# Scaling softmax blocks out of the score bank, and one float32 product with v per head and key block in two column groups

## The chip, the cores and the metric

The kernel runs on one core of a Trainium2 chip. The core has five engines with queues of their own: TensorE (PE, with weight loads shown apart as PEld), VectorE (DVE), ScalarE (ACT), GpSimd (POOL) and SyncE (SP, which issues the transfers here). PE writes its products to PSUM, eight banks of 128 partitions x 512 float32 numbers; everything else lies in SBUF. The metric is the time of one execution on the device in microseconds (us).

## The reference

Two layers of a decoder trunk on 512 positions of width 1024, all float32. Layer 0 has stick-breaking attention, layer 1 forgetting attention; each is followed by a gated MLP with a short convolution.

```python
for i in range(DEPTH):                       # 2 layers; i = 0 stick-breaking, i = 1 forgetting
    h = modulate(rmsnorm(x, g_mix_pre[i]), sh_a, sc_a)
    q, k, v = split(h @ w_qkv[i])            # 16 heads of 64
    # i = 0: a = sigmoid(z) * prod over later keys of (1 - sigmoid(z)), strictly causal
    # i = 1: a = softmax(z + cum[t] - cum[s]), causal, cum = cumsum(log_sigmoid(h @ w_fg + b_fg))
    o = (a @ v) @ w_o[i]
    x = x + gt_a * rmsnorm(o, g_mix_post[i])
    h = modulate(rmsnorm(x, g_ffn_pre[i]), sh_f, sc_f)
    y = (silu(conv3(h @ w_gate[i])) * (h @ w_up[i])) @ w_down[i]
    x = x + gt_f * rmsnorm(y, g_ffn_post[i])
```

The modulation vectors come from `silu(c) @ w_mod[i] + b_mod[i]`.

## The kernel before

Most products are made of three (`mm3`): both operands are kept as a rounded high half and a low half of type float32r, and high x high, low x high and high x low are added in a bank. `split` makes the halves: ACT copies (the high half), DVE or POOL subtracts (the low half).

Attention goes head by head. For each of the four blocks of 128 queries (`qb` from 3 to 0, so 512, 384, 256 and 128 keys wide), `scores` makes two products into a bank `ps`. Layer 0 then calls `stick`, layer 1 `fox`: DVE adds the decay and takes the row's minimum (L461), ACT takes the exponential and its sum (L464), DVE the reciprocal (L465) and the scaling (L466). In `fox` all of it after the first step lies in an SBUF tile `fx`.

One head later, `transposed` turns the probabilities with PE into banks `pa`, one for each key block `kb` (512, 384, 256 and 128 queries wide), and `split` brings each to SBUF as `ah` and `al`. `weighted` then multiplies: for each key block two products, with `ah` and with `al` moving and a tile of v as the fixed operand that holds 64 columns of high halves and 64 of low halves of this head. So high and low parts of the result stand in the two halves of the bank `po`; ACT copies one half across (L496), DVE adds the other (L497), and after the second head of a pair `split` makes `oh` and `ol`.

The order on PE and SP is as written. Where the attention would wait, `fill` puts pieces of other products (projections `pqk` of the next pair, values `pv`, output projections into further `po` banks) between its steps; the table `UNITS` has how many pieces a head takes. In layer 0 also pieces of the modulation stand there: L202 makes eight float32 products, 32 columns each, at four column positions of the array. Within ACT, DVE and POOL a scheduler sets the order in the attention stages. All PSUM tiles come from one pool of eight banks, and most working tiles in SBUF from one pool of 44 slots.

Of the kernel before, what the change touches and what calls it, by code (L numbers as in the profile page):

```python
# [20 lines left out]
NH = 16  # L21
HD = 64
# [6 lines left out]
MULN = 256  # L29
# [8 lines left out]
def trunk(ctx, tc, x, c, w_mod, b_mod, g_mix_pre, g_mix_post, w_qkv, w_o, w_fg, b_fg,  # L38
          g_ffn_pre, g_ffn_post, w_gate, w_up, w_conv, b_conv, w_down, out):
    nc = tc.nc  # L40
# [22 lines left out]
    def tiny(s, n=1):  # L63
        return sb.tile([P, n], F32, tag=f"tiny{n}", name=nm(s), bufs=24)
# [180 lines left out]
    def split(hi, lo, src, engine=None):  # L245
        nc.scalar.copy(hi, src)  # L246
        (engine or nc.vector).tensor_tensor(lo, src, hi.bitcast(F32), op=ALU.subtract)  # L247
# [158 lines left out]
    A, B = slice(0, HD), slice(HD, P)  # L406
# [30 lines left out]
    def scores(l, hd, qb, q, k):  # L437
        n = (qb + 1) * P
        qs = slice(qb * P, n)
        ps = bank("ps")  # L440
        for i in range(2):
            nc.tensor.matmul(ps[:, :n], q[hd][:, qs], k[hd][i][:, :n], start=i == 0, stop=i == 1)  # L442
        return ps, n
# [11 lines left out]
        return bt  # L455

    def fox(ps, qb, cum):
        n = (qb + 1) * P
        t = slot("fx", F32)
        m, s, r = tiny("mx"), tiny("sm"), tiny("rc")  # L460
        nc.vector.tensor_tensor_reduce(  # L461
            t[:, :n].rearrange("p (b k) -> p b k", k=P), ps[:, :n].rearrange("p (b k) -> p b k", k=P), cum(qb),
            1.0, BIG, op0=ALU.add, op1=ALU.min, accum_out=m)
        nc.scalar.activation(t[:, :n], t[:, :n], AF.Exp, scale=-1.0, bias=m, accum_out=s)  # L464
        nc.vector.reciprocal(r, s)  # L465
        nc.vector.tensor_scalar(t[:, :n], t[:, :n], r, None, op0=ALU.mult)  # L466
        return t

    def transposed(probs):

        res = {}
        for kb in range(NT):
            n = (NT - kb) * P
            ps = bank("pa")
            for qb in range(NT - 1, kb - 1, -1):
                nc.tensor.transpose(ps[:, (qb - kb) * P : (qb - kb + 1) * P], probs[qb][:, kb * P : (kb + 1) * P], idn)  # L476
            if kb == 1:
                shared = slot("ah"), slot("al")
            hi, lo = (slot("ah"), slot("al")) if kb in (0, 2) else shared
            o = 384 if kb == 3 else 0  # L480
            hi, lo = hi[:, o : o + n], lo[:, o : o + n]
            split(hi, lo, ps[:, :n])
            res[kb] = (hi, lo)
            yield res

    def weighted(h, vt, at, o):

        po = bank("po")
        for kb in range(NT):
            lhs = by_head(vt[h // 4, kb])[:, h % 4, :]  # L490
            nc.tensor.matmul(po[:, kb * P :], lhs, at[kb][0], start=kb == 0, stop=False)
            nc.tensor.matmul(po[:, kb * P :], lhs, at[kb][1], start=False, stop=kb == NT - 1)
            yield
        hi, lo, f = o
        own, other = ((A, B), (B, A))[h % 2]
        nc.scalar.copy(f[own], po[other])  # L496
        nc.vector.tensor_tensor(f[own], po[own], f[own], op=ALU.add)  # L497
        if h % 2:
            split(hi, lo, f)

    def by_head(v):

        return v.rearrange("p (h e) -> p h e", h=4)

    def values(l, g, t, ht, vt):

# [70 lines left out]
    def drain(g):  # L577
        for _ in g:
            pass

    def attention(l, qk, vt, ot, filler, units, bg):


        get = cums_of.get(l)
        late, cums = None, {}
        for h in range(NH + 1):
            p, hd = divmod(h, 2)
            done = [0, 0]

            def fill(n=1):  # L590
                done[0] += n
                u = (units[h] * min(done[0], 12) + 11) // 12 - done[1]
                done[1] += u
                filler.run(u)

            if h < NH and hd == 0:
                ot.append((slot("oh"), slot("ol"), slot("of", F32)))
# [4 lines left out]
            probs, at = {}, None  # L602
# [12 lines left out]
            if late:  # L615
                drain(turned)
                for i, _ in enumerate(weighted(late[1], vt, at, ot[late[1] // 2])):
                    if i % 2:
                        fill()
            fill(12)  # L620
            late = (probs, h)
            if h:
                bg.step()


    def begin(vt, qk):
# [41 lines left out]
        part, xt, acc, H = {}, {}, [], S // 2  # L668
# [87 lines left out]
        r = stats(0)  # L756
# [4 lines left out]
        for t in range(NT):  # L761
            n = t + 1
# [29 lines left out]
        for j in range(ND):  # L792
            n = j + 1
# [17 lines left out]
        qk[0, 0] = queries(acc[4], 0.125)  # L811
        qk[0, 1] = keys(acc[6], kl[0])
        ws.upto(1)
        for g in range(2):
            for t in range(NT):
                keep_values(acc[t][:, 256 * g : 256 * g + 256], g, t, vt)
        qk[1, 0] = queries(acc[5], 0.125)
        return ht

# [1 line left out]
    for l in range(DEPTH):  # L821
        bg = Background([(l, GT_A), (l, SC_F), (l, SH_F)] if l == 0 else [], mod_part_pe)
        scale = -0.125 if l % 2 else 0.125
# [33 lines left out]
        gens, ot = [], []  # L857
        for p in range(1, NPAIR):
            if (l, p) == (0, 3):
                gens.append(conv_columns())  # L860
            gens += [proj(l, p, j, ht, s, qk) for j, s in ((0, scale), (1, None)) if (p, j) not in qk]
            if p % 2 == 0 and (p // 2, 0) not in vt:
# [66 lines left out]
        for f in range(2, NF):  # L929
            g, u = bank("pgu"), bank("pgu")  # L930
# [67 lines left out]
```

## Time and profile before

| | |
|---|---|
| runs, median of 3 (lowest to highest) | 1297.1 us (1296.88 to 1300.71) |
| profiled execution | 1298.38 us |
| span in its profile | 1296.6 us |
| mean granted PE clock | 0.993 |
| PE, PEld busy | 1254.0, 1050.5 us |
| DVE, ACT, POOL busy | 783.0, 621.3, 269.8 us |
| attention of layer 0, of layer 1 | about 70 to 262 us, 690 to 910 us of the span |

A row of groups reads: line, engine, operation, output <- inputs, shapes, count | busy us, mean ns of one | idle time of the engine before them, and what ended it. A row of a timeline reads: start in us, us, engine, line, operation, tiles, shapes, count, and in brackets the idle time before it and what ended it. Idle time counts where the engine that sets the end has it.

### The profile page before, as it was taken

What the parts mean: (1) busy time and instruction counts of PE and PEld (TensorE: products, weight loads), DVE (VectorE), ACT (ScalarE), POOL (GpSimd) and SP (SyncE); (2) the same over time, 40 slices, a digit from 0 to 9 for tenths busy, and PEclk for the clock granted to TensorE, in tenths of its full rate; (3) what the DMA queues carried; (4) which work ended last, traced back from release to release, by engine and by line L of the source; (5) the groups of instructions that cost most, each with busy time, mean ns of one, the idle gap of its engine ahead of it and who ended that gap; (6) DMA issues with size and microseconds to landing.
All of it is one profiled execution on the core that took longest, in us unless ns stands there. A gap on an engine that the chain in (4) does not pass through costs nothing.

```text
span 1296.6 us, 17226 instructions
## 1 busy us (share of the span) xinstructions
PE 1254.0 (97%) x6348; PEld 1050.5 (81%) x6348; DVE 783.0 (60%) x1397; ACT 621.3 (48%) x1185; POOL 269.8 (21%) x302
## 2 busy tenths in 40 slices
PE   4999999999999999999999899999999999999997
PEld 3787888789887888888887879878888888888886
DVE  7776776666688987422365767786685444442233
ACT  5586676665333334311466555566743333332121
POOL 4674444610000000000216444453100000000000
PEclk9999999999999999999999999999999999999999
DMA  8654524223576865323405242322263333333331
GB/s 275 200 163 133 192 98 163 82 82 126 174 257 219 280 206 168 98 98 98 132 1 165 82 130 82 114 98 82 65 228 98 97 97 98 98 98 98 98 98 65
DMA packets 178359, 169.72 MB, mean 131 GB/s; under 512 B 6984, under 2 KB 151776, under 8 KB 178275
## 3 DMA queue, kind: packets, MB, share of 16 engines
q1 hardware_dynamic: 178098, 168.56, 41.2%
q8 instruction: 50, 0.82, 0.3%
q14 instruction: 35, 0.28, 0.1%
q10 hardware_dynamic: 176, 0.07, 0.0%
HBM read 166.44 MB, written 2.16 MB: 130 GB/s over the span
## 4 chain that ended last, share of the span: by engine, by line
PE 80%; DVE 9%; ACT 4%; DMA 3%; issue 2%; SPq 1%; POOL 1%; POOLq 0%; DVEq 0%; ACTq 0%
PE pgu L321 12%; PE pgu L322 12%; PE pgu L320 12%; PE pd L321 6%; PE pd L322 6%; PE pd L320 6%; PE pqk L320 3%; PE pqk L321 3%; PE pqk L322 3%; PE ps L442 3%; PE pa L476 2%; PE pv L320 2%; PE pv L321 2%; PE pv L322 2%; DVE fx L466 2%
## 5 line engine op out<-in xcount | busy, mean ns | idle before, releaser
L246 ACT CAST wh<-wf 128x1024 fp32r<-128x1024 f32 (+2 forms) x178 | 185.2, 1041 | 311.4 <-PE pd L322 134.6
L247 DVE TENSOR_TENSOR wl<-wf,wh 128x1024 fp32r<-128x1024 f32 x122 | 149.2, 1223 | 218.2 <-ACT wh L246 215.9
L321 PE MATMUL pgu<-htl,wh 128*128 128x512 f32 (+1 forms) x736 | 276.4, 376 | 0.3 <-DVE htl L382 0.3
L320 PE MATMUL pgu<-hth,wh 128*128 128x512 f32 (+1 forms) x736 | 276.3, 375 | 0.0
L322 PE MATMUL pgu<-hth,wl 128*128 128x512 f32 (+1 forms) x736 | 276.2, 375 | 0.0
L321 PEld LDWEIGHTS pgu<-htl,wh 128*128 128x128 f32 x736 | 138.5, 188 | 25.7 <-DVE htl L382 0.6
L320 PEld LDWEIGHTS pgu<-hth,wh 128*128 128x128 f32 x736 | 138.5, 188 | 25.0
L322 PEld LDWEIGHTS pgu<-hth,wl 128*128 128x128 f32 x736 | 138.5, 188 | 25.0
L247 POOL TENSOR_TENSOR wl<-wf,wh 128x1024 fp32r<-128x1024 f32 (+3 forms) x56 | 130.2, 2329 | 130.2 <-ACT wh L246 120.6
L320 PE MATMUL pd<-wh,yh 128*128 128x512 f32 x288 | 112.0, 389 | 0.0
L321 PE MATMUL pd<-wl,yh 128*128 128x512 f32 x288 | 112.0, 389 | 0.0
L322 PE MATMUL pd<-wh,yl 128*128 128x512 f32 x288 | 112.0, 389 | 0.0
L333 POOL TENSOR_TENSOR r<-v,mhalf 128x1 f32<-128x1 f32 x32 | 17.8, 557 | 447.7 <-DVE v L329 447.7
L320 PE MATMUL pqk<-hth,wh 128*128 128x512 f32 (+1 forms) x240 | 100.0, 417 | 0.0
L322 PE MATMUL pqk<-hth,wl 128*128 128x512 f32 (+1 forms) x240 | 93.7, 390 | 0.5 <-POOL wl L247 0.5
L321 PE MATMUL pqk<-htl,wh 128*128 128x512 f32 (+1 forms) x240 | 93.4, 389 | 0.0
L910 ACT ACTIVATE cv<-cv 128x512 f32<-128x512 f32 x44 | 27.8, 633 | 108.6 <-DVE cv L909 100.8
L146 DVE SCALAR_TENSOR_TENSOR acc<-wm,csil,acc 128x1024 f32<-128x1024 f32 x52 | 66.6, 1280 | 12.4 <-DMA wm<-in_w_mod_dram 12.1
L320 PE MATMUL pv<-wh,hth 128*128 128x256 f32 (+1 forms) x224 | 69.8, 311 | 0.8 <-ACT hth L717 0.4
L321 PE MATMUL pv<-wl,hth 128*128 128x256 f32 (+1 forms) x224 | 66.8, 298 | 1.2 <-POOL wl L247 1.2
L322 PE MATMUL pv<-wh,htl 128*128 128x256 f32 (+1 forms) x224 | 66.9, 299 | 1.0 <-DVE htl L722 1.0
L320 PEld LDWEIGHTS pd<-wh,yh 128*128 128x128 f32 x288 | 54.1, 188 | 11.3
(212 smaller groups left out, 2456.4 us busy)
## 6 DMA issues: line engine op xcount, KB each, us to landing
wm<-in_w_mod_dram SPq DMA_DIRECT2D x80, 512.0 KB, 5.2
wf<-in_w_ffn_gate_dram SPq DMA_DIRECT2D x44, 512.0 KB, 4.7
wf<-in_w_ffn_up_dram SPq DMA_DIRECT2D x44, 512.0 KB, 4.3
wf<-in_w_ffn_down_dram SPq DMA_DIRECT2D x44, 512.0 KB, 3.4
wf<-in_w_qkv_dram SPq DMA_DIRECT2D x41, 512.0 KB, 5.0
wm<-in_w_mod_dram SPq DMA_DIRECT2D x32, 256.0 KB, 4.5
wf<-in_w_o_dram SPq DMA_DIRECT2D x16, 512.0 KB, 4.0
cum<-cumd SPq DMA_DIRECT2D x16, 512.0 KB, 4.2
```

Source lines behind the costliest of these rows:

```text
L146: nc.vector.scalar_tensor_tensor(acc, w, csil[:, d : d + 1], acc, op0=ALU.mult, op1=ALU.add)
L246: nc.scalar.copy(hi, src)
L247: (engine or nc.vector).tensor_tensor(lo, src, hi.bitcast(F32), op=ALU.subtract)
L320: nc.tensor.matmul(ps, ah, bh, start=first, stop=False)
L321: nc.tensor.matmul(ps, ah, bl, start=False, stop=False)
L322: nc.tensor.matmul(ps, al, bh, start=False, stop=last)
L333: nc.gpsimd.tensor_tensor(r, v, mhalf, op=ALU.pow)
L442: nc.tensor.matmul(ps[:, :n], q[hd][:, qs], k[hd][i][:, :n], start=i == 0, stop=i == 1)
L466: nc.vector.tensor_scalar(t[:, :n], t[:, :n], r, None, op0=ALU.mult)
L476: nc.tensor.transpose(ps[:, (qb - kb) * P : (qb - kb + 1) * P], probs[qb][:, kb * P : (kb + 1) * P], idn)
L910: nc.scalar.activation(a, a, AF.Silu)
```

## The change

Softmax (`fox`, layer 1): blocks of 256 and 128 columns are no longer written to SBUF by the first step. The sum with the decay and the exponential go back into the score bank, and the scaling reads the bank and writes the SBUF tile. Blocks of 512 and 384 stay as they were. A score bank of the narrower blocks is now in use until the scaling.

Product with v (both layers): the turned probabilities are copied to SBUF once, as float32 (`at`, ACT alone), v is kept as float32 (ACT alone), and the product of each head and key block is one float32 product. It is made for a pair of heads at once, every other head: head 0 to partitions 0 to 63 of the bank, head 1 to 64 to 127, each in a column group of its own. The bank then holds the pair's result, and `split` makes `oh` and `ol` from it. The fill steps that stood within the product are gone; what they ran comes in the fill step behind it.

```diff
     def fox(ps, qb, cum):
         n = (qb + 1) * P
-        t = slot("fx", F32)
+        t = slot("fx", F32)[:, :n]
+        e = t if n > MULN else ps[:, :n]
...
-        nc.scalar.activation(t[:, :n], t[:, :n], AF.Exp, scale=-1.0, bias=m, accum_out=s)
+        nc.scalar.activation(e, e, AF.Exp, scale=-1.0, bias=m, accum_out=s)
         nc.vector.reciprocal(r, s)
-        nc.vector.tensor_scalar(t[:, :n], t[:, :n], r, None, op0=ALU.mult)
+        nc.vector.tensor_scalar(t, e, r, None, op0=ALU.mult)
...
             if kb == 1:
-                shared = slot("ah"), slot("al")
-            hi, lo = (slot("ah"), slot("al")) if kb in (0, 2) else shared
+                shared = slot("at", F32)
+            t = shared if kb % 2 else slot("at", F32)
             o = 384 if kb == 3 else 0
-            hi, lo = hi[:, o : o + n], lo[:, o : o + n]
-            split(hi, lo, ps[:, :n])
-            res[kb] = (hi, lo)
+            res[kb] = t[:, o : o + n]
+            nc.scalar.copy(res[kb], ps[:, :n])
...
-    def weighted(h, vt, at, o):
+    def weighted(p, vt, at, o):
         po = bank("po")
         for kb in range(NT):
-            lhs = by_head(vt[h // 4, kb])[:, h % 4, :]
-            nc.tensor.matmul(po[:, kb * P :], lhs, at[kb][0], start=kb == 0, stop=False)
-            nc.tensor.matmul(po[:, kb * P :], lhs, at[kb][1], start=False, stop=kb == NT - 1)
-            yield
-        hi, lo, f = o
-        own, other = ((A, B), (B, A))[h % 2]
-        nc.scalar.copy(f[own], po[other])
-        nc.vector.tensor_tensor(f[own], po[own], f[own], op=ALU.add)
-        if h % 2:
-            split(hi, lo, f)
+            for hd in range(2):
+                e = P * (p % 4) + HD * hd
+                nc.tensor.matmul(po[HD * hd : HD * hd + HD, kb * P :], vt[p // 4, kb][:, e : e + HD], at[hd][kb],
+                                 start=kb == 0, stop=kb == NT - 1, tile_position=(0, HD * hd))
+        split(*o, po)
...
     def keep_values(ps, g, t, vt):
-        vt[g, t] = slot("v")
-        dst = by_head(vt[g, t])
-        split(dst[:, :, :HD], dst[:, :, HD:], ps.rearrange("p (h e) -> p h e", h=4))
+        if (g // 2, t) not in vt:
+            vt[g // 2, t] = slot("v", F32)
+        o = 256 * (g % 2)
+        nc.scalar.copy(vt[g // 2, t][:, o : o + 256], ps)
...
                 if turned:
-                    at = next(turned)
+                    ats[late[1] % 2] = next(turned)
                     fill()
             fill(2)
...
             if late:
                 drain(turned)
-                for i, _ in enumerate(weighted(late[1], vt, at, ot[late[1] // 2])):
-                    if i % 2:
-                        fill()
+                if hd == 0:
+                    weighted(p - 1, vt, ats, ot[p - 1])
+                    ats = {}
             fill(12)
```

The start of layer 0 stores its values with four ACT copies in the same way, without subtractions.

PE, at the first product with v in layer 1, of one head and with one fill step (`pqk`) inside, before:

```order
L491 MATMUL po_6892<-ah_6796,v_6349 128x512
L492 MATMUL po_6892<-al_6797,v_6349 128x512
L491 MATMUL po_6892<-ah_6821,v_6401 128x384
L492 MATMUL po_6892<-al_6822,v_6401 128x384
L320 MATMUL pqk_6875<-hth_6016,wh_6723 128x512
L321 MATMUL pqk_6875<-htl_6017,wh_6723 128x512
L322 MATMUL pqk_6875<-hth_6016,wl_6724 128x512
L491 MATMUL po_6892<-ah_6845,v_6490 128x256
L492 MATMUL po_6892<-al_6846,v_6490 128x256
L491 MATMUL po_6892<-ah_6821,v_6557 128x128
L492 MATMUL po_6892<-al_6822,v_6557 128x128
```

The first product there now is that of the pair, one head later (`at_6539` and its like are of the first head, `at_6659` and its like of the second):

```order
L493 MATMUL po_6776<-at_6539,v_6097 64x512
L493 MATMUL po_6776<-at_6659,v_6097 64x512
L493 MATMUL po_6776<-at_6562,v_6148 64x384
L493 MATMUL po_6776<-at_6700,v_6148 64x384
L493 MATMUL po_6776<-at_6584,v_6236 64x256
L493 MATMUL po_6776<-at_6728,v_6236 64x256
L493 MATMUL po_6776<-at_6562,v_6302 64x128
L493 MATMUL po_6776<-at_6700,v_6302 64x128
```

Sixteen products of two heads are now eight, in turn for the two heads, with nothing between them.

DVE, at the end of the first head in layer 1 whose turned probabilities that product takes, from the scaling of the 256-wide block on, before (`fx` the softmax, `pa` the bank of the turned block, ISA the step of L461):

```order
L466 TENSOR_SCALAR fx_6831<-fx_6831,rc_6834 128x256
L247 TENSOR_TENSOR al_6846<-pa_6842,ah_6845 128x256
L461 ISA fx_6855,mx_6856<-ps_6852,cum_6636 128x128
L461 ISA mx_6856 128x1
L465 RECIPROCAL rc_6858<-sm_6857 128x1
L466 TENSOR_SCALAR fx_6855<-fx_6855,rc_6858 128x128
L415 SCALAR_TENSOR_TENSOR qa_6863<-pqk_6766,qa_6863 64x512
L415 SCALAR_TENSOR_TENSOR qb_6864<-pqk_6766,qb_6864 64x512
L247 TENSOR_TENSOR al_6822<-pa_6879,ah_6821 128x128
L497 TENSOR_TENSOR of_6631<-po_6892,of_6631 64x512
```

and now:

```order
L468 TENSOR_SCALAR fx_6570<-ps_6567,rc_6573 128x256
L463 ISA ps_6589,mx_6593<-ps_6589,cum_6379 128x128
L463 ISA mx_6593 128x1
L467 RECIPROCAL rc_6595<-sm_6594 128x1
L468 TENSOR_SCALAR fx_6592<-ps_6589,rc_6595 128x128
L415 SCALAR_TENSOR_TENSOR qa_6600<-pqk_6509,qa_6600 64x512
L415 SCALAR_TENSOR_TENSOR qb_6601<-pqk_6509,qb_6601 64x512
```

The subtractions and the join are gone from the queue, and the two scalings read a bank.

ACT now, at the end of the head before the pair's product (`at_6700` is the tile that its last product takes; L466 is now the exponential):

```order
L484 COPY at_6700<-pa_6696 128x384
L466 ACTIVATE ps_6708,sm_6713<-ps_6708,mx_6712 128x256
L512 COPY v_6097<-pv_6689 128x256
L484 COPY at_6728<-pa_6725 128x256
L466 ACTIVATE ps_6736,sm_6741<-ps_6736,mx_6740 128x128
L484 COPY at_6700<-pa_6755 128x128
L512 COPY v_6148<-pv_6748 128x256
L246 CAST oh_6373<-po_6776 128x512
```

Each copy that the product needs stands behind an exponential of the running head. Before, the copies to `ah` stood among the exponentials in the same way.

More of the change, by code (lines that the diff above doesn't have):

```diff
@@ L458, in fox @@
         n = (qb + 1) * P
-        t = slot("fx", F32)
+        t = slot("fx", F32)[:, :n]
+        e = t if n > MULN else ps[:, :n]
         m, s, r = tiny("mx"), tiny("sm"), tiny("rc")
         nc.vector.tensor_tensor_reduce(
-            t[:, :n].rearrange("p (b k) -> p b k", k=P), ps[:, :n].rearrange("p (b k) -> p b k", k=P), cum(qb),
+            e.rearrange("p (b k) -> p b k", k=P), ps[:, :n].rearrange("p (b k) -> p b k", k=P), cum(qb),
             1.0, BIG, op0=ALU.add, op1=ALU.min, accum_out=m)
-        nc.scalar.activation(t[:, :n], t[:, :n], AF.Exp, scale=-1.0, bias=m, accum_out=s)
+        nc.scalar.activation(e, e, AF.Exp, scale=-1.0, bias=m, accum_out=s)
         nc.vector.reciprocal(r, s)
-        nc.vector.tensor_scalar(t[:, :n], t[:, :n], r, None, op0=ALU.mult)
+        nc.vector.tensor_scalar(t, e, r, None, op0=ALU.mult)
         return t
@@ L584, in attention @@
         get = cums_of.get(l)
-        late, cums = None, {}
+        late, ats, cums = None, {}, {}
         for h in range(NH + 1):
@@ L601, in attention @@
                         cums[i] = get(i)
-            probs, at = {}, None
+            probs = {}
             turned = transposed(late[0]) if late else None
@@ L813, in begin @@
         ws.upto(1)
-        for g in range(2):
-            for t in range(NT):
-                keep_values(acc[t][:, 256 * g : 256 * g + 256], g, t, vt)
+        for t in range(NT):
+            vt[0, t] = slot("v", F32)
+            nc.scalar.copy(vt[0, t], acc[t])
         qk[1, 0] = queries(acc[5], 0.125)
@@ L861, in trunk @@
             gens += [proj(l, p, j, ht, s, qk) for j, s in ((0, scale), (1, None)) if (p, j) not in qk]
-            if p % 2 == 0 and (p // 2, 0) not in vt:
+            if p % 2 == 0 and p >= (4 if l == 0 else 2):
                 gens += [values(l, p // 2, t, ht, vt) for t in range(NT)]
```

4 lines of the change are left out of this document (1 added, 3 removed).

## The prediction

> **What bounds the kernel now.** I read the page first, for the engine that sets the end.
>
> ```profile
> PE 1254.0 (97%) x6348; PEld 1050.5 (81%) x6348; DVE 783.0 (60%) x1397; ACT 621.3 (48%) x1185; POOL 269.8 (21%) x302
> PE 80%; DVE 9%; ACT 4%; DMA 3%; issue 2%; SPq 1%; POOL 1%; POOLq 0%; DVEq 0%; ACTq 0%
> ```
>
> TensorE (PE) is busy 97% of the span and 80% of the chain that ended last. So the change can act in two ways only: by the PE time of the products with v, and by the PE's idle stretches and clock inside the two attention stages. The table of windows shows these stages (columns: busy us and count for PE, PEld, DVE, ACT, POOL; then granted clock, DMA share, GB/s), and three short stretches inside the second one, with a fourth for contrast.
>
> ```profile
> 70.00:262.00 192.00, 188.90 (x1122) 155.58 (x1121) 133.65 (x245) 135.58 (x295) 99.07 (x139) 1.00 0.42 138
> 690.00:910.00 220.00, 209.02 (x1171) 179.00 (x1169) 156.88 (x396) 131.25 (x302) 101.54 (x82) 0.98 0.36 112
> ...
> 723.00:726.50 3.50, 3.50 (x12) 2.87 (x11) 2.29 (x6) 1.86 (x4) 0.00 (x0) 0.52 0.12 36
> 825.50:829.00 3.50, 3.50 (x11) 2.72 (x10) 1.38 (x3) 1.22 (x2) 1.43 (x2) 0.51 0.94 298
> 873.50:877.00 3.50, 3.50 (x15) 2.93 (x13) 1.75 (x5) 2.60 (x6) 3.18 (x3) 0.53 0.20 39
> ...
> 774.00:777.50 3.50, 3.50 (x22) 2.99 (x21) 1.91 (x5) 2.00 (x4) 0.20 (x1) 1.00 0.34 102
> ```
>
> Layer 0's attention (70 to 262) leaves PE idle for 192.00 - 188.90 = 3.1 us, layer 1's (690 to 910) for 220.00 - 209.02 = 11.0 us. Layer 1 also has three stretches of 3.5 us at about half clock, in which (0.48 + 0.49 + 0.47) x 3.5 = 5.0 us of PE work are lost. Next, who ends the idle time: the PE groups of 690 to 910 by shape (last column: idle before, and what ended it), and one row of the table of waits for 70 to 262.
>
> ```profile
> L492 PE MATMUL po<-al,v 128*128 128x256 f32 x16 | 4.7, 294 | 1.1 <-DVE al L247 1.1
> L492 PE MATMUL po<-al,v 128*128 128x128 f32 x16 | 4.7, 292 | 5.6 <-DVE al L247 5.6
> L491 PE MATMUL po<-ah,v 128*128 128x128 f32 x16 | 3.8, 235 | 1.9 <-ACT ah L246 1.9
> ...
> PE po L491 <- DVE om L453: 1.2, 1, 1.2
> ```
>
> So 1.1 + 5.6 + 1.9 = 8.6 of the 11.0 us stand in front of the last products of a head, mostly for the low half `al`, the DVE subtraction of `split`. The timeline of one such place, PE, then DVE, then POOL, says why it is late, and the last row is a shorter stall elsewhere:
>
> ```profile
> 719.06 0.33 PE L491 MATMUL po<-ah,v 128*128 128x128 f32 x1 [1.21 <-ACT ah L246]
> 721.58 0.33 PE L492 MATMUL po<-al,v 128*128 128x128 f32 x1 [2.19 <-DVE al L247]
> ...
> 718.13 0.16 DVE L465 RECIPROCAL rc<-sm 128x1 f32<-128x1 f32 x1 [0.99 <-ACT fx L464]
> 718.33 1.47 DVE L466 TENSOR_SCALAR fx<-fx,rc 128x128 f32<-128x128 f32 x1
> 719.81 0.69 DVE L415 SCALAR_TENSOR_TENSOR qa<-pqk,qa 64x512 fp32r<-64x512 f32 x1
> 720.51 0.69 DVE L415 SCALAR_TENSOR_TENSOR qb<-pqk,qb 64x512 fp32r<-64x512 f32 x1
> 721.23 0.29 DVE L247 TENSOR_TENSOR al<-pa,ah 128x128 fp32r<-128x128 f32 x1
> ...
> 717.36 2.35 POOL L247 TENSOR_TENSOR wl<-wf,wh 128x1024 fp32r<-128x1024 f32 x1 [1.67 <-issue]
> ...
> 773.68 0.33 PE L492 MATMUL po<-al,v 128*128 128x128 f32 x1 [1.31 <-DVE al L247]
> ```
>
> The 128-wide scaling L466 takes 1.47 us and ends at 719.80; POOL's subtraction, which reads and writes SBUF as it does, ran from 717.36 to 719.71. Behind it wait two query pieces and then the subtraction PE needs. PE stood still for 1.21 + 2.19 = 3.4 us, and from 723 its clock was halved. After the stall of 1.31 us at 773.68 the clock stayed at 1.00: short stalls did not cost it.
>
> **The change, part by part.** *DVE and ACT.* Groups of 690 to 910:
>
> ```profile
> L466 DVE TENSOR_SCALAR fx<-fx,rc 128x256 f32<-128x256 f32 x16 | 14.0, 873 | 0.2
> L466 DVE TENSOR_SCALAR fx<-fx,rc 128x128 f32<-128x128 f32 x16 | 12.2, 761 | 0.5
> ...
> L461 DVE CUSTOM_DVE_ANT_1 fx<-ps,cum 128x256 f32<-128x256 f32 x16 | 6.6, 414 | 0.3 <-issue 0.3
> L461 DVE CUSTOM_DVE_ANT_0 fx<-ps,cum 128x128 f32<-128x128 f32 x16 | 4.4, 273 | 0.0
> ...
> L497 DVE TENSOR_TENSOR of<-po,of 64x512 f32<-64x512 f32 x16 | 11.0, 687 | 14.5 <-ACT of L496 14.4
> L247 DVE TENSOR_TENSOR al<-pa,ah 128x512 fp32r<-128x512 f32 x16 | 11.0, 687 | 1.9 <-ACT ah L246 1.9
> L247 DVE TENSOR_TENSOR al<-pa,ah 128x384 fp32r<-128x384 f32 x16 | 8.8, 552 | 0.2
> L247 DVE TENSOR_TENSOR al<-pa,ah 128x256 fp32r<-128x256 f32 x16 | 6.7, 417 | 0.1
> L247 DVE TENSOR_TENSOR al<-pa,ah 128x128 fp32r<-128x128 f32 x16 | 4.5, 282 | 0.7 <-ACT ah L246 0.6
> ```
>
> The subtractions `al` go (11.0 + 8.8 + 6.7 + 4.5 = 31.0 us), and so do the joins L497 (11.0 us), at which DVE's queue also stood for 14.5 us, since a join waits for an ACT copy of PE's product. The scalings of 256 and 128 columns move to the score bank. No row shows a scaling out of a bank. Its nearest rows read the same bank in the same widths, 0.414 and 0.273 us; if the wait beside POOL stayed, it would be 0.873 and 0.761. I take the lower ends: the `al` rows, also out of a bank, have means of 0.417 and 0.282, so nothing much lengthens them while POOL works the same stage. That is 16 x (0.873 - 0.414) + 16 x (0.761 - 0.273) = 15.1 us less. Together DVE falls from 156.9 to about 100 us in the stage. None of this counts by itself; it counts where PE waited. PE's product now needs only the ACT copy `at`, not the copy and a subtraction behind it.
>
> What comes back in layer 1: the 8.6 us in front of the products, less what ACT still holds up. ACT's own part was 1.9 us. With the subtraction gone its bounds are 0 and, if every wait on `al` were really for the copy ahead of it, 8.6; the copy in the place above was late by 1.21 of the 3.4 us. I keep 1.0 us, near the low end, since a pair's product waits once for two heads and works on its wider blocks first (2 x 0.43 x 1152 / 512 = 1.9 us by the rounds below) before it needs the last one. So 7.6 us. The three half-clock stretches follow the long stalls; with them gone I take all 5.0 us (bounds 0 and 5.0). In layer 0 the one wait of 1.2 us is of a product bank for a scan on DVE; half as many product banks are asked for, and DVE loses the same 16 sets of subtractions there, so I take 0.6 (bounds 0 and 3.1, all the idle time of that stage).
>
> *The products on PE.* Before: eight products of a head, uninterrupted, and the first PE row behind them.
>
> ```profile
> 895.32 0.39 PE L491 MATMUL po<-ah,v 128*128 128x512 f32 x1
> 895.55 0.40 PE L492 MATMUL po<-al,v 128*128 128x512 f32 x1
> ...
> 896.43 0.27 PE L492 MATMUL po<-al,v 128*128 128x128 f32 x1
> 896.54 0.44 PE L320 MATMUL po<-wh,oh 128*128 128x512 f32 x1
> ```
>
> That is 1.22 us a head, 2.44 a pair; a 512-wide product is followed after 0.23 us (895.32 to 895.55), the last 128-wide one after 0.11 (896.43 to 896.54). After: eight float32 products, one per head and key block, in two groups of 64 columns. The trace has float32 products in groups: L202, eight of them, 512 wide, in four groups of 32 columns, on PE and on its weight loads.
>
> ```profile
> 100.12 0.27 PE L492 MATMUL po<-al,v 128*128 128x128 f32 x1
> 100.33 1.92 PE L202 MATMUL pm<-wm,c 128*32 128x512 f32 x16
> 102.18 0.50 PE L442 MATMUL ps<-kh,qb 128*128 128x512 f32 x1
> 102.52 0.39 PE L442 MATMUL ps<-kl,qb 128*128 128x512 f32 x1
> ...
> 100.78 0.13 PEld L202 LDWEIGHTS pm<-wm,c 128*32 128x32 f32 x4 [0.30 <-issue]
> 101.21 0.13 PEld L202 LDWEIGHTS pm<-wm,c 128*32 128x32 f32 x4 [0.30 <-issue]
> ```
>
> Each product is two records (x16 for eight), and loads come in fours, 0.43 us apart: a round of 512 columns takes 0.43 us for all groups at once. A pair then needs two rounds for each of 512 + 384 + 256 + 128 = 1280 columns: 2 x 0.43 x 1280 / 512 = 2.15 us, if two groups run together as four do. Going in and out costs: from 100.12 to 100.33 it is 0.21 and not 0.11, so 0.10 more; the four rounds would end at 102.05 and PE goes on at 102.18, 0.13 more; the next step, to 102.52, is 0.34 and not 0.23, 0.11 more. So 2.15 + 0.10 + 0.13 + 0.11 = 2.49 against 2.44, and 16 pairs make +0.8 us. If the groups ran one after another, a pair would take 2.15 us more, +34.4 us in all; that is the other bound. [...]
>
> The value pieces lose a subtraction each, and the pair's result is split out of the bank directly; both are DVE and ACT work that PE covers.
>
> **The sum.** -7.6 - 5.0 - 0.6 + 0.8 = -12.4 us, of the profiled execution's 1298.38 (span 1296.6, 1.8 us around it): 1286.0. The median of the runs is 1297.1, 1.3 lower, and so the forecast is 1284.7.
>
> **The rivals.** *The wait moves to ACT.* The copies `at` of a head's last blocks stand in ACT's order behind the exponentials, and those wait for DVE's minima, which stand behind 512- and 384-wide scalings still in SBUF beside POOL. If half of the 8.6 us returns in that form (4.3, of which the forecast has 1.0) and one half-clock stretch stays (1.7): -12.4 + 3.3 + 1.7 = -7.4, so 1289.7. For it: the order. Against it: three fill steps of PE lie between the last transposes and the product, and the last copy is needed only 1.9 us into that. This also covers scalings that still wait for POOL.
>
> *The two groups run in turn.* One mechanism, at L493, price +34.4: 1284.7 + 34.4 = 1319. It decides the sign once a pair takes over 0.8 us more than now. Against it are the rounds of four above; for it only that no row shows two groups of 64.
>
> *Score banks held longer.* A 128-wide block's bank was free when DVE had its minimum, 0.99 us ahead of the reciprocal at 718.13, at 717.14; now it is free when it is scaled, at 719.80 in that place or, without POOL's part, near 718.6. Scores could wait for a bank at the end of a layer, when output projections hold four to six of the eight. Two blocks of three heads, 1.5 to 2 us each, twice: about 10 to 12 us, and the time is 1296, no change.
>
> *More comes back.* All idle time of both stages (11.0 + 3.1) and the clock (5.0): 1297.1 - 19.1 = 1278.
>
> **Chances.** Forecast 0.60 (its own range 1280 to 1290), wait on ACT 0.16, more 0.08, banks 0.08, groups in turn 0.08. The range from 1278 to 1293 takes in the first three. A measurement of this kernel tells 0.3%, 3.9 us, from no change: faster means under 1293.2. Forecast, ACT and more (0.84) lie there but for 0.02; that 0.02 and 0.06 of the bank case are no change, the other 0.02 of it and the groups in turn are slower. So 0.82 faster, 0.08 the same, 0.10 slower.
>
> **What would show it.** Right: a product group of a pair takes 2.1 to 2.3 us of PE; idle time in front of it under 2 us in layer 1's attention; granted clock 1.00 throughout that stage; scalings of 256 and 128 near 0.41 and 0.28 us; DVE near 100 us there. Wrong: rounds of one group at a time (over 4 us a pair), idle time before scores or transposes ended by the scaling of a bank, or waits of the same size ended by the ACT copy.

## The result, and the profile after

The changed kernel takes 1279.95 us in the median of 4 runs (1278.2 to 1282.74), beside 1296.99 for the kernel before in the runs it is compared with. The ratio is 0.9866, 95% interval 0.9838 to 0.9894: faster, by 17.0 us or 1.3%. The forecast was 1284.7 with a range from 1278 to 1293. The profiled execution took 1280.88 us with a span of 1279.1; all comparisons of traces below are with the span of 1296.6 before, 17.5 us more.

The page of the changed kernel, parts 1 and 4:

```profile
PE 1244.3 (97%) x6348; PEld 1024.9 (80%) x6348; DVE 694.3 (54%) x1205; ACT 600.1 (47%) x1149; POOL 267.4 (21%) x302
...
PE 81%; DVE 8%; DMA 5%; ACT 3%; issue 2%; POOL 1%; SPq 1%; DVEq 0%; ACTq 0%; POOLq 0%
```

PE is still what bounds the kernel. DVE has lost 88.7 us of work, but that is not the gain. Where the gain lies is read from four rows of PE's timeline in each kernel: the first scores and the first product of the MLP's gate, in layer 0 and in layer 1. Before:

```profile
71.00 0.39 PE L442 MATMUL ps<-kh,qa 128*128 128x512 f32 x1
...
289.78 0.28 PE L320 MATMUL pgu<-hth,wh 128*128 128x256 f32 x1
...
691.84 0.50 PE L442 MATMUL ps<-kh,qa 128*128 128x512 f32 x1 [1.44 <-POOL kh L433]
...
926.30 0.28 PE L320 MATMUL pgu<-hth,wh 128*128 128x256 f32 x1
```

After:

```profile
71.56 0.39 PE L442 MATMUL ps<-kh,qa 128*128 128x512 f32 x1
...
287.33 0.28 PE L320 MATMUL pgu<-hth,wh 128*128 128x256 f32 x1
...
690.16 0.50 PE L442 MATMUL ps<-kh,qa 128*128 128x512 f32 x1 [1.44 <-POOL kh L433]
...
908.93 0.28 PE L320 MATMUL pgu<-hth,wh 128*128 128x256 f32 x1
```

From scores to gate, layer 0 takes 215.77 us instead of 218.78 (3.0 less) and layer 1 218.77 instead of 234.46 (15.7 less). Between 287.33 and 690.16 the changed kernel takes 0.8 us more (402.83, not 402.06), but the run below with the product alone takes 401.79 there, so that is scatter and no cost of the change. The windows of the two attention stages, the shares of time as before, and all that PE waited for in layer 1's:

```profile
70.00:262.00 192.00, 190.38 (x1135) 146.61 (x1134) 95.16 (x150) 127.37 (x276) 100.48 (x141) 1.00 0.44 140
688.00:891.00 203.00, 199.50 (x1165) 163.53 (x1164) 107.39 (x302) 118.33 (x286) 99.03 (x81) 1.00 0.39 120
```

```profile
PE pqk L322 <- POOL wl L247: 1.5, 1, 1.5
PE ps L442 <- POOL kh L433: 1.4, 1, 1.4
PE ps L442 <- ACT at L484: 0.4, 1, 0.4
PE po L493 <- ACT at L484: 0.2, 1, 0.2
```

In layer 1 the granted clock is 1.00 and not 0.98: the three half-clock stretches are gone. PE's idle time is 3.5 us and not 11.0, and 0.2 us of it stands in front of a product with v, where 8.6 stood. The product of a pair, on PE:

```profile
96.83 0.39 PE L322 MATMUL pqk<-hth,wl 128*128 128x512 f32 x1
97.15 2.37 PE L493 MATMUL po<-at,v 128*64 128x512 f32 x16
99.45 0.50 PE L320 MATMUL pqk<-hth,wh 128*128 128x512 f32 x1
99.79 0.40 PE L321 MATMUL pqk<-htl,wh 128*128 128x512 f32 x1
```

It takes 2.30 us from its start to the next product's, with 0.09 us more than a step's usual 0.23 ahead of it and 0.11 more behind it: 2.50 us, against 2.49 in the forecast. And the scalings, in layer 1's attention:

```profile
L468 DVE TENSOR_SCALAR fx<-fx,rc 128x512 f32<-128x512 f32 x16 | 13.8, 860 | 0.4
L468 DVE TENSOR_SCALAR fx<-fx,rc 128x384 f32<-128x384 f32 x16 | 11.5, 717 | 0.2
...
L468 DVE TENSOR_SCALAR fx<-ps,rc 128x256 f32<-128x256 f32 x16 | 7.7, 482 | 0.3
L468 DVE TENSOR_SCALAR fx<-ps,rc 128x128 f32<-128x128 f32 x16 | 5.6, 351 | 0.6
```

### The profile page after: what moved, and what is told of

Same layout as the page of the kernel before. It is cut to its first block, busy times and chain, and to the rows that moved or that the text cites. A ratio compares the mean times of both kernels' runs of the same rounds, so it can differ in the third digit from the quotient of the medians.

```text
span 1279.1 us, 17003 instructions
## 1 busy us (share of the span) xinstructions
PE 1244.3 (97%) x6348; PEld 1024.9 (80%) x6348; DVE 694.3 (54%) x1205; ACT 600.1 (47%) x1149; POOL 267.4 (21%) x302
## 4 chain that ended last, share of the span: by engine, by line
PE 81%; DVE 8%; DMA 5%; ACT 3%; issue 2%; POOL 1%; SPq 1%; DVEq 0%; ACTq 0%; POOLq 0%
PE pgu L321 11%; PE pgu L322 11%; PE pgu L320 11%; PE pd L322 6%; PE pd L320 6%; PE pd L321 6%; PE pqk L320 4%; PE pqk L321 4%; PE pqk L322 4%; PE ps L442 3%; PE po L493 3%; PE pa L478 3%; PE pv L320 2%; PE pv L322 2%; PE pv L321 2%; DMA wm<-in_w_mod_dram 2%
## 5 line engine op out<-in xcount | busy, mean ns | idle before, releaser
L146 DVE SCALAR_TENSOR_TENSOR acc<-wm,csil,acc 128x1024 f32<-128x1024 f32 x52 | 66.6, 1280 | 14.2 <-DMA wm<-in_w_mod_dram 13.7
L321 PEld LDWEIGHTS pd<-wl,yh 128*128 128x128 f32 x288 | 54.1, 188 | 11.3
```

The lines of the kernel that those rows point to most:

```text
L146: nc.vector.scalar_tensor_tensor(acc, w, csil[:, d : d + 1], acc, op0=ALU.mult, op1=ALU.add)
L321: nc.tensor.matmul(ps, ah, bl, start=False, stop=False)
```

## The experiments

Two changes are made at once, and either could be what ended PE's waits. Theory at first: a scaling in SBUF stands beside POOL, and the subtraction `al` that PE needs stands behind it. Rivals: DVE's load and joins; the later product of a pair; the cheaper product itself.

### Each half of the change alone

The softmax alone (kernel before, with the new `fox`):

```diff
-        t = slot("fx", F32)
+        t = slot("fx", F32)[:, :n]
+        e = t if n > MULN else ps[:, :n]
...
```

> The kernel before with the change of the softmax alone: blocks of 256 and 128 columns stay in the score bank until they are scaled; the product with v, its two halves and their DVE subtractions are as before. Theory (the scaling that stands beside POOL is what makes the subtraction late): the scalings take about 0.48 and 0.35 us instead of 0.87 and 0.76, PE's idle time in front of the last products in layer 1 falls from 8.6 us to under 4, at least two of the three half-clock stretches go, and the time is about 1289 us. Rival (the subtractions and the join themselves, in DVE's queue, make it late): idle time stays at 7 us or more and the time is 1295 to 1297 us.

1286.86 us, ratio 0.9924 (0.9906 to 0.9941). Scalings as in the changed kernel (0.480 and 0.344 us), no half-clock stretch, and in front of the last products:

```profile
L494 PE MATMUL po<-al,v 128*128 128x256 f32 x16 | 4.8, 303 | 0.2 <-DVE al L247 0.2
L494 PE MATMUL po<-al,v 128*128 128x128 f32 x16 | 4.6, 286 | 0.0
L493 PE MATMUL po<-ah,v 128*128 128x128 f32 x16 | 3.5, 222 | 0.0
```

The idle time there fell from 8.6 to 0.2 us, though every subtraction and join stayed. The theory holds, and by more than it had promised (about 1289 us).

The product alone (changed kernel, with the old `fox`):

```diff
-        t = slot("fx", F32)[:, :n]
-        e = t if n > MULN else ps[:, :n]
+        t = slot("fx", F32)
...
```

> The changed kernel with the softmax as before: all four blocks in SBUF from the first step on, scaled there. Theory (the product needs only an ACT copy now, so a late scaling no longer reaches it): idle time in front of the products under 1.5 us in layer 1, no half-clock stretch in its attention, time within 2 us of the changed kernel, 1280 to 1282 us. Rival (the exponentials behind which the copies stand wait for minima that stand behind blocked scalings, so the scaling in the bank is needed as well): 4 us or more of idle time in front of the products, ended by ACT copies, and 1286 to 1290 us.

1280.69 us, ratio 0.9875 (0.9855 to 0.9894), not to be told from the changed kernel's 0.9866. Scalings and waits:

```profile
L466 DVE TENSOR_SCALAR fx<-fx,rc 128x128 f32<-128x128 f32 x16 | 15.0, 940 | 0.6
L466 DVE TENSOR_SCALAR fx<-fx,rc 128x256 f32<-128x256 f32 x16 | 14.7, 921 | 0.3
```

```profile
PE pa L476 <- DVE fx L466: 1.6, 2, 1.0
PE pqk L322 <- POOL wl L247: 0.8, 1, 0.8
```

The scalings are slower than before, and yet PE waits in front of none of the products with v; for the scalings themselves it waits 1.6 us in all. So the halves do not add: 0.76% and 1.25% alone, 1.34% together. The stages say it more plainly. From scores to gate, layer 1 takes 222.0 us with the softmax alone, 219.4 with the product alone and 218.8 with both, beside 234.5 before. Layer 0, which has no `fox`, takes 218.6, 215.7 and 215.8, beside 218.8: its gain is the product's. Each half breaks the same chain in layer 1; at which link, the runs below ask.

### All four blocks in the bank

```diff
-        e = t if n > MULN else ps[:, :n]
+        e = ps[:, :n]
```

> The changed kernel with all four softmax blocks in the score bank until scaled, 512 and 384 columns too. Scalings of 512 and 384 should fall from 0.86 and 0.72 us to near 0.70 and 0.56. Theory (PE no longer waits for DVE in front of the products, so faster scalings bring nothing): 1279 to 1281 us. Rival (four banks held until the scaling are too many): idle time of PE before scores or transposes, ended by a scaling, of 5 us or more, and 1285 us or more.

1278.6 us, ratio 0.9858 (0.9837 to 0.9879). Scalings of 512 and 384 fell to 0.749 and 0.615 us, and the longest total that PE waited in layer 1 was 1.4 us, for POOL's `kh`, as long as in the changed kernel. Four banks held are not too many, and faster scalings bring nothing that the intervals can tell.

### Where the two column groups overlap

```diff
-        for kb in range(NT):
-            for hd in range(2):
+        for hd in range(2):
+            for kb in range(NT):
```

> The changed kernel with the eight products of a pair in another order: the four of the first head, then the four of the second, still in two column groups. If the array runs what is next in the program and only neighbours of different groups overlap, a pair takes near 4.3 us instead of 2.3, and the time is about 1280 + 16 x 2 = 1312 us. If it takes products of another free group ahead of their turn, a pair stays near 2.3 to 2.6 us and the time near 1280 to 1284 us.

1303.93 us, ratio 1.0057 (1.0039 to 1.0074), 24 us more than the changed kernel. A pair on PE:

```profile
97.04 3.93 PE L493 MATMUL po<-at,v 128*64 128x512 f32 x16
100.89 0.50 PE L320 MATMUL pqk<-hth,wh 128*128 128x512 f32 x1
```

3.85 us and not 2.30, 1.55 more; 16 times that is 24.8, the whole difference. The same products in the same groups overlapped here only around the seam between the heads. PE's weight loads come singly and then, at the seam, six close together:

```profile
98.27 0.14 PEld L493 LDWEIGHTS po<-at,v 128*64 128x64 f32 x1 [0.18 <-issue]
98.59 0.62 PEld L493 LDWEIGHTS po<-at,v 128*64 128x64 f32 x6 [0.19 <-issue]
```

The seam was wider than two neighbours. By the trace's single records the first product of the second head (512 columns) starts at 98.60, 0.01 us behind the third of the first head (256, at 98.59), and before the fourth (128, at 99.02), which the program has ahead of it; all 16 pairs have this order. It came out between the two expectations, nearer the first. A rival of the prediction, groups in turn, is thus not what this kernel does, but it is one exchange of two loops away.

### DVE back in front of the product

Copies of the turned probabilities by DVE, with the new softmax, then with the old one:

```diff
-            nc.scalar.copy(res[kb], ps[:, :n])
+            nc.vector.tensor_copy(res[kb], ps[:, :n])
```

> The changed kernel with the copies of the turned probabilities made by DVE instead of ACT, so that PE's product waits for DVE's queue again, while the scalings of 256 and 128 columns stay in the bank and pairs stay as they are. Theory (what made DVE late was the scaling beside POOL, and a pair's product leaves slack): idle time in front of the products under 2 us, time within 3 us of the changed kernel, 1279 to 1283 us. Rival (any wait of the product for DVE's queue stalls PE): 5 us or more of idle time there and 1286 us or more.

1280.67 us, ratio 0.9873 (0.9859 to 0.9888); 0.6 us of waiting in front of the products (0.5 in the longest group, ended by a DVE copy). As the theory had it.

> As the run before it, with the copies on DVE, but the softmax blocks all in SBUF and scaled there, as before the change. Theory (blocked scalings reach PE when its product stands behind DVE): idle time in front of the products of 4 us or more again, at least one half-clock stretch in layer 1's attention, and 1286 to 1292 us. Rival (making the product of a pair at once, one head later, is what gives PE its slack): no more idle time than in the run before it, and the same time within 2 us.

1280.6 us, ratio 0.9868 (0.9852 to 0.9884), and no wait for a product. Here the first theory fell: the product stands behind DVE, and DVE's scalings stand beside POOL as before (0.736 us for 128 columns, 0.958 for 256), and PE does not wait. So something else in the product's change gives the slack. Three candidates: the pair's product comes later; the joins are gone from DVE's queue; a copy is one step where `ah` and `al` were two.

Without the later product: as in the run before, but the product of each head in its own head.

```diff
...
-                if hd == 0:
-                    weighted(p - 1, vt, ats, ot[p - 1])
-                    ats = {}
+                if hd == 1:
+                    po = bank("po")
+                weighted(late[1], vt, ats[late[1] % 2], po, ot[late[1] // 2])
```

> The run with copies on DVE and all scalings in SBUF, with one more step back: the float32 product of each head is made in its own head again, in its column group alone, not with the other head of its pair. PE then works 1.5 to 2 us more for each pair (24 to 34 us in all), so the waits are to be read, not the time. Theory (that the product of a pair comes one head later is the slack): idle time in front of the products in layer 1 is 3 us or more again, ended by DVE's copies. Rival (it is the joins, the second subtraction and the values' subtractions, gone from DVE's queue, that ended the waits): idle time under 1 us.

1319.3 us, ratio 1.0174 (1.0155 to 1.0193): each head's product alone now takes what a pair took (2.30 us on PE, from 100.30 to 102.60 at one place in layer 0). The waits, which the run was made for:

```profile
L490 PE MATMUL po<-at,v 128*64 128x512 f32 x32 | 17.2, 618 | 0.0
...
L490 PE MATMUL po<-at,v 128*64 128x128 f32 x32 | 6.1, 273 | 0.0
```

None, so the later product is not what is needed; PE's slower pace here may help a little, which this run does not separate. But the timeline of DVE at the first head of layer 1, the place that the prediction showed, says what happened:

```profile
734.12 0.29 DVE L482 COPY at<-pa 128x128 f32<-128x128 f32 x1
735.30 0.16 DVE L465 RECIPROCAL rc<-sm 128x1 f32<-128x1 f32 x1 [0.89 <-ACT fx L464]
735.50 1.36 DVE L466 TENSOR_SCALAR fx<-fx,rc 128x128 f32<-128x128 f32 x1
736.89 0.69 DVE L415 SCALAR_TENSOR_TENSOR qa<-pqk,qa 64x512 fp32r<-64x512 f32 x1
737.59 0.69 DVE L415 SCALAR_TENSOR_TENSOR qb<-pqk,qb 64x512 fp32r<-64x512 f32 x1
```

Apart from the copies, the instructions are those of the kernel before, and the scaling is as slow (1.36 us; 1.47 before). But the copy of the last block stands ahead of the reciprocal, the scaling and the query pieces, where the subtraction stood behind them all. A copy needs PE alone; the subtraction needed ACT's copy too, and the scheduler had put it four places later. That is 4 us of queue. Before, ACT's copy was itself late in ACT's queue: it ended at 719.01, so 2.2 of the 4 us, to 721.23, are the subtraction's wait in DVE's queue alone.

### The last block's halves, earlier in DVE's queue

Kernel before, with the high half of the last block made by DVE as well, so that its subtraction waits for no other engine:

```diff
-            split(hi, lo, ps[:, :n])
+            if kb == NT - 1:
+                nc.vector.tensor_copy(hi, ps[:, :n])
+                nc.vector.tensor_tensor(lo, ps[:, :n], hi.bitcast(F32), op=ALU.subtract)
+            else:
+                split(hi, lo, ps[:, :n])
```

> The kernel before with one change: of each head's last turned block (128 columns) DVE makes the high half too, so its subtraction no longer waits for an ACT copy. In DVE's order both then stand ahead of the last scaling's reciprocal and of the query pieces, where the subtraction stood behind them. All scalings stay in SBUF, joins, product and order of PE stay. DVE works 16 x 0.28 us more in layer 1. Theory (the subtraction is late by its place in DVE's queue, behind the blocked scaling): idle time in front of the products under 3 us, at most one half-clock stretch, 1286 to 1290 us. Rival (DVE's load as a whole makes it late, and its place matters little): 6 us or more of idle time, 1294 to 1298 us.

1290.52 us, ratio 0.9947 (0.993 to 0.9965): half a microsecond over the range expected. DVE now has, at the same head, the copy and the subtraction ahead of the reciprocal:

```profile
718.13 0.29 DVE L483 CAST ah<-pa 128x128 fp32r<-128x128 f32 x1
718.45 0.29 DVE L484 TENSOR_TENSOR al<-pa,ah 128x128 fp32r<-128x128 f32 x1
719.21 0.16 DVE L465 RECIPROCAL rc<-sm 128x1 f32<-128x1 f32 x1 [0.46 <-ACT fx L464]
719.40 1.52 DVE L466 TENSOR_SCALAR fx<-fx,rc 128x128 f32<-128x128 f32 x1
```

Scalings are as slow as before (0.862 and 0.755 us), and PE's groups in front of the last products:

```profile
L496 PE MATMUL po<-al,v 128*128 128x128 f32 x16 | 4.7, 293 | 1.2 <-DVE al L484 1.1
L496 PE MATMUL po<-al,v 128*128 128x256 f32 x16 | 4.6, 288 | 0.9 <-DVE al L247 0.9
...
L495 PE MATMUL po<-ah,v 128*128 128x128 f32 x16 | 3.8, 235 | 0.8 <-DVE ah L483 0.8
```

8.6 us of idle time became 2.9, and one of three half-clock stretches is left. DVE does more work than before and PE waits less. The edit does two things at once, though: it moves the subtraction ahead in DVE's queue, and it takes the copy `ah` of that block out of ACT's queue, for which PE had waited 1.9 of the 8.6 us. This run does not part them.

### POOL's part, the joins, and a later product

POOL's subtractions for the weights in pieces of 256 columns, kernel before:

```diff
+        step = 256 if engine is nc.gpsimd and len(src.shape) == 2 and src.shape[1] in (512, 1024) else src.shape[-1]
...
+            for c in range(0, src.shape[1], step):
+                engine.tensor_tensor(lo[:, c : c + step], src[:, c : c + step], hi[:, c : c + step].bitcast(F32), op=ALU.subtract)
```

> The kernel before with one change: POOL's subtractions for the weights, one of 1024 or 512 columns, are made in pieces of 256. Theory (a scaling in SBUF waits for the POOL instruction that runs, to its end): the scalings of 256 and 128 columns take under 0.6 us in the mean instead of 0.87 and 0.76, the idle time in front of the products falls from 8.6 us to under 5, and the time is 1287 to 1293 us. Rival (the scaling is slow for another reason, or POOL holds it for all of its work): means over 0.75 us, idle time 7 us or more, 1295 to 1298 us.

1288.37 us, ratio 0.9934 (0.9921 to 0.9947).

```profile
L471 DVE TENSOR_SCALAR fx<-fx,rc 128x256 f32<-128x256 f32 x16 | 8.7, 542 | 0.2
...
L471 DVE TENSOR_SCALAR fx<-fx,rc 128x128 f32<-128x128 f32 x16 | 5.7, 359 | 0.5
```

```profile
PE po L497 <- DVE al L252: 1.9, 4, 0.7
```

The scalings of 256 and 128 fell from 0.873 and 0.761 us, and the wait for `al` to 1.9 us with no wait of more than 0.7. POOL does all of its work as before, only in shorter instructions (it is busy 294.2 us in all, not 269.8). So a scaling in SBUF waited here for the POOL instruction that ran, and it was the length of that instruction that reached PE. The trace before agrees: of the 16 scalings of 128 columns five took over 0.4 us, 1.37 to 2.24, and each of the five ended 0.08 us after a subtraction of POOL.

Without the join (for even heads the part of the result from the low half of v is left out, for odd heads the part from the high half):

```diff
-        nc.scalar.copy(f[own], po[other])
-        nc.vector.tensor_tensor(f[own], po[own], f[own], op=ALU.add)
+        nc.scalar.copy(f[own], po[own])
```

> The kernel before without the join: ACT copies the head's own half of the product's bank and DVE's addition of the other half (L497) is left out, so the part of the result from the low half of v is left out. Theory (the join, at which DVE's queue stands 14.5 us for ACT, passes its delay on to the subtractions that PE needs): idle time in front of the products falls from 8.6 us to under 4, at most one half-clock stretch, 1286 to 1291 us. Rival (the subtractions are late by the scalings beside POOL alone): 7 us or more of idle time, 1294 to 1298 us.

1294.08 us, ratio 0.9978 (0.9966 to 0.999). In front of the last products 6.4 us are left:

```profile
L492 PE MATMUL po<-al,v 128*128 128x128 f32 x16 | 4.7, 292 | 4.8 <-DVE al L247 4.8
...
L491 PE MATMUL po<-ah,v 128*128 128x128 f32 x16 | 3.8, 235 | 1.6 <-ACT ah L246 1.6
```

A small part: nearer the rival than the theory, and between the two in time. The 14.5 us for which DVE stood at the joins were mostly time that nobody needed.

The product of a head moved behind all fill steps, kernel before:

```diff
-                for i, _ in enumerate(weighted(late[1], vt, at, ot[late[1] // 2])):
-                    if i % 2:
-                        fill()
             fill(12)
+            if late:
+                drain(weighted(late[1], vt, at, ot[late[1] // 2]))
```

> The kernel before with the product of a head moved behind all fill steps of its head, the two that stood inside it too. The last block's halves are then needed about 0.5 us later than before, the first block's about 1.2 us later. Theory (slack): the waits for the last block of 1 to 2.5 us shorten by about 0.5 us each, eight of them, idle time 5 to 6 us instead of 8.6 and one or two half-clock stretches, 1289 to 1293 us. Rival (a late DVE queue stays late): 8 us or more of idle time, 1296 to 1299 us.

1293.97 us, ratio 0.9975 (0.996 to 0.999): 5.7 us of idle time left in front of the products (3.9, 0.8 and 1.0), two half-clock stretches. The waits shortened about as expected, but the time fell by 1 us less than the range had it; half a microsecond of slack is not enough against 4 us of queue.

### A try at the remaining waits

The changed kernel with the copy of the key halves on DVE:

```diff
-            nc.gpsimd.tensor_scalar(hi[other], hi[own].bitcast(F32), 1.0, 1.0, op0=ALU.mult, op1=ALU.mult)
+            nc.vector.tensor_scalar(hi[other], hi[own].bitcast(F32), 1.0, 1.0, op0=ALU.mult, op1=ALU.mult)
```

> The changed kernel with the copy of the high key halves to the other half of the partitions (L433) on DVE instead of POOL. In the changed kernel's trace PE waits for this copy before the first scores of layer 1 (1.4 us) and for a POOL subtraction of weights (1.5 us). Expected with DVE's new slack: both waits fall, 1 to 4 us less than the changed kernel, 1276 to 1279 us. Rival (DVE's scalings stand beside POOL anyway and the copy reads SBUF too): no change within 1.5 us.

1281.39 us, ratio 0.988 (0.9865 to 0.9895): no gain. The wait for POOL's subtraction fell from 1.5 to 0.4 us, but the one before the first scores stayed at 1.1 us, now for DVE, and other waits of 0.3 to 0.6 us came. No variant beats the changed kernel by more than the intervals; all four blocks in the bank is at least as fast.

## Why the prediction was right, and where its sizes were off

*The bound and the place* were right: PE, its idle time in front of the products in layer 1, and the half clock behind it. 15.7 of the 17.5 us came back in layer 1's attention.

*The half clock* was counted at 5.0 us, all of it to return, and all three stretches are gone in the changed kernel, as in both halves alone.

*Idle time in front of the products* was the term that was mis-sized. The forecast took 8.6 us from the column of idle time and kept 1.0 for ACT: 7.6. What is left is 0.2. But the column also counts less than such a wait costs. It begins when the product ahead has ended, and that product, in its record, runs longer than its step: at the place shown, 721.58 comes 2.52 us after 719.06, where the step is 0.06 when nothing waits (100.06 to 100.12 in the same trace), so 2.46 us were lost to the 2.19 in brackets. Summed over all steps from start to start on PE's timeline, the products with v of layer 1 took 30.23 us before and 19.02 after, 11.2 less, of which the shorter product itself is 8 x (2.44 - 2.30) = 1.1. So some 10 us of waiting came back, not 7.6. Counted in this way, the products with v of layer 1 took 21.54 us with the softmax alone, 22.52 with POOL in quarters, 24.10 with the last block on DVE, 26.88 with the product later and 27.56 without the join: the order in which the runs' times fall, but 2 us are still lost in the first of them, where the column has 0.2. The other steps of the stage took 4.5 us less in the changed kernel. The half clock's 5.0 are the main part of that, less one longer wait for POOL's `wl` (1.5 us, 0.5 before) and the switches of the pairs; the rest was not taken apart.

*Layer 0* was mis-sized too: forecast 0.6 back and 0.4 for half of the pairs, measured 3.0 less. The forecast had taken one wait of five in the table (1.2, 0.7, 0.4, 0.3 and 0.3 us), that of the product bank for a scan; in the changed kernel only one wait of that table is left, and it is a new one:

```profile
PE ps L442 <- POOL kh L433: 1.6, 1, 1.6
```

All waits for DVE's scans, subtractions and value pieces are gone. By steps, the products with v of layer 0 took 21.92 us before and 18.43 after, 3.5 less, of which 1.1 are again the shorter product; the other steps took 0.5 more in sum, and the switches of the pairs are among them.

*The product* was right in size: 2.49 forecast for a pair with its switches, 2.50 measured, against 2.44. The forecast took it that two groups run together as the four of L202 did, whose 16 records of 0.43 us took 1.85 us (100.33 to 102.18 in the kernel before), 3.7 of 4. Two groups came near that here: 2.30 us stand beside the 2.15 of full overlap.

*The scalings* came out at 0.482 and 0.351 us, not 0.414 and 0.273: between the two bounds, near the one taken, and DVE had 107 us of work in the stage, not 100. It did not matter, for the second run shows that this half of the change added nothing measurable to the other.

*The reason for the late subtraction* was half told. The forecast had it behind the scaling and the query pieces, and put the delay down to the scaling. The runs show three links, each of which breaks the chain: POOL's long instruction (in quarters: 9 us back), the scaling's place in SBUF (in the bank: 9 us back), and the subtraction's place in DVE's queue behind that scaling (moved ahead, with ACT's copy out of the way too: 7 us back, at the same scalings). The change broke the last two.

*The rivals.* The wait did not move to ACT (0.2 us). Banks held longer cost 0 to 0.4 us, or 0.5 with all four; the 10 to 12 us that the forecast had for them do not follow from its words as they stand, for two blocks of three heads at 1.5 to 2 us are 9 to 12 us, and twice that is 18 to 24. Groups in turn is real as a mechanism, and its price was measured at 24 us for the order that brings it about; the forecast's 34.4 was for no overlap at all. *More comes back*, at 1278, is two microseconds from the result, nearer than the forecast at 1284.7, and the result lies 0.05 under the forecast's own range (1280 to 1290). But not all idle time came back, as that rival had it: 1.6 and 3.5 us of it are left in the two stages, and the time is made up by what the column of idle time had not counted.

What stays open: how much of the slack in the run without the later product is PE's slower pace, what the joins and the second subtraction each add beside the queue's order, and what DVE's order does without the change on ACT. No run has the kernel before with only its products made later by a whole head.

## What to carry to other kernels

When PE waits for a short instruction on another engine, look at what stands ahead of it in that queue, and ask whether it needs to stand there: here an instruction with one producer was put four places earlier than one with two, and with it there PE waited less (2.9 us in front of the products, not 8.6), at more work for DVE. Five of 16 scalings of 128 columns on DVE, between SBUF tiles, ended here 0.08 us after POOL's running instruction, at 1.37 to 2.24 us each, so long POOL instructions were a hidden part of DVE's queue: look at them too. And write float32 products of different column groups next to each other, in turn: head by head, they overlapped here only around the seam, and a pair took 3.85 us, not 2.30.

## What the runs showed that I had not expected

In these traces the half clock does not follow from a wait's length. PE waits 1.44 us before the first scores of layer 1 in most of these kernels, at a granted clock of 1.00 behind it in the kernels before and after. With POOL's subtractions in quarters the same wait stands at 692.66, and PE's clock behind it is half (rows of the table of windows; the clock is the third value from the end):

```profile
692.66 0.50 PE L447 MATMUL ps<-kh,qa 128*128 128x512 f32 x1 [1.44 <-POOL kh L438]
```

```profile
690.63:694.04 3.41, 1.92 (x8) 1.04 (x7) 2.06 (x3) 1.16 (x2) 1.23 (x2) 1.00 0.36 98
694.04:697.45 3.41, 3.41 (x10) 2.85 (x9) 0.00 (x0) 1.99 (x2) 0.83 (x2) 0.50 0.97 289
```

The prediction had said that short stalls did not cost clock; here one did. In the granted clock of the kernel before, the half-clock stretches begin at 723.16, 825.56 and 873.35 us, 102.40 and 47.79 apart, which are 30 and 14 times the 3.413 us that each lasts. So it might count where in a step of that length a stall falls; this is a guess from these numbers, and the two stalls do not bear it out. Set back from 723.16 in such steps, the step around the harmless stall before is

```profile
689.03:692.44 3.41, 1.92 (x9) 1.03 (x7) 2.20 (x5) 1.16 (x2) 1.20 (x2) 1.00 0.11 29
```

and that stall (690.40 to 691.84) lies whole inside that step, as the costly one (691.22 to 692.66) lies inside 690.63 to 694.04. In both steps PE is busy for 1.92 of 3.41 us by its records. What decides between the two stays open. A stall of 1.4 us in PE thus cost 1.4 us in one run and 1.4 + 1.7 in another, by an estimate from the rows above (half of 3.41 us at a clock of 0.50). The count of three stretches is that of one execution, too: over the executions of the kernel before, the mean granted clock goes from 0.990 to 0.997.

The two halves of the change, each worth 9 and 16 us alone, are worth 17 together: a stall that needs several causes goes when any one of them goes, and its gain can be booked only once.
